# A batched matrix product: stores in 6 KB pieces, matmuls half by half in every group, and five stores queued behind the last load

## The chip, the cores and the metric

The kernel runs on one core of a Trainium2 chip. The metric is device time in microseconds (us) of one execution, the median of several runs. A profile of one execution shows what each engine did: TensorE (PE) multiplies, VectorE (DVE) and ScalarE (ACT) work on elements, and SyncE (SP) issues the transfers (DMAs) between HBM and the on-chip memory SBUF, which 16 DMA engines carry out.

## The reference

```python
dim: batch 32, i 256, j 512, k 384, all float32
def reference(x, y):        # x [32, 256, 512], y [32, 512, 384]
    return np.einsum('bij,bjk->bik', x, y).astype(np.float32)
```

So 32 independent products of a 256 x 512 matrix by a 512 x 384 matrix. Read are 16.8 MB of x and 25.2 MB of y, written are 12.6 MB.

## The kernel before

The 32 batches go in N = 8 groups of Q = 4. In SBUF each batch of a group has 32 of the 128 partitions. x arrives with 8 rows of a batch in each partition (16 KB in one piece), y with 16 rows (24 KB in one piece); only the y of the last group is loaded in four parts, with pieces of 6 KB.

A group goes through these steps. `transpose_x` casts x to float16 on VectorE (L83) and transposes it in 32 x 32 blocks of 4-byte words, two float16 values each (L90, L96). `round_y` casts y to float16 on VectorE in four parts of four rows (L102). `multiply` runs 128 matmuls (L113): the four batches lie on four row strips of TensorE, each sums over 16 steps t, and a group has two halves e (128 of the 256 output rows). Each half of a batch has a PSUM bank of its own, so a group uses all eight. `collect` copies a bank to the output tile (L128), and `store` writes that tile to HBM (L137).

The width decides the layout of the output. With WIDE, in groups 0 to 5, a batch has 32 output partitions with 8 output rows each: one store of 1.5 MiB a group, in pieces of 12 KB, and four copies of 32 partitions for each bank. With NARROW, in groups 6 and 7, a batch has 64 partitions with 4 rows: two stores of 0.75 MiB a group, in pieces of 6 KB, and two copies of 64 partitions for each bank.

In the wide groups the first half is multiplied in full, then the second, and ScalarE copies behind each half, except the last bank, whose copies VectorE makes in the next group. In groups 6 and 7 the halves alternate by quarters of t, and the copies follow at the end, on ScalarE; half of those of group 7 are on VectorE.

All loads and stores are issued from SP, in the order in which the program writes them. There are two buffers each for x, for the transposed x, for y and for the rounded y, and five for the output (DEFER + 2). A load waits until the buffer that it overwrites has been read: x(n+3) for the cast of x(n+1), y(n+2) for the rounding of y(n). The order of each engine is the program's order (`keep`). Around the end SP issues: x6, y5 and S2 (the store of group 2), x7, y6 and S3, y7 and S4, then S5, S6, S7.

Of the kernel before, what the change touches and what calls it, by code (L numbers as in the profile page):

```python
# [1 line left out]

# [4 lines left out]


MM_DT = mybir.dt.float16
F32 = mybir.dt.float32  # L10
P = 128


Q = 4
WIDE = 32
NARROW = 64

DEFER = 3

STEP = 4  # L20


@with_exitstack
def kernel(
    ctx: ExitStack,
    tc: tile.TileContext,
    x: bass.AP,
    y: bass.AP,
    out: bass.AP,
):  # L30
    nc = tc.nc

    B, I, J = x.shape
    _, _, K = y.shape

    PQ = P // Q
    R = I // PQ
    T = J // PQ
    TW = T // 2
    NE = I // P  # L40
    N = B // Q

    x_pool = ctx.enter_context(tc.tile_pool(name="x_pool", bufs=2))
    y_pool = ctx.enter_context(tc.tile_pool(name="y_pool", bufs=2))
    xr_pool = ctx.enter_context(tc.tile_pool(name="xr_pool", bufs=1))
    xt_pool = ctx.enter_context(tc.tile_pool(name="xt_pool", bufs=2))
    yr_pool = ctx.enter_context(tc.tile_pool(name="yr_pool", bufs=2))
    o_pool = ctx.enter_context(tc.tile_pool(name="o_pool", bufs=DEFER + 2))
    psum_pool = ctx.enter_context(
        tc.tile_pool(name="psum", bufs=2 * Q, space=bass.MemoryType.PSUM)  # L50
    )

    keep = tc.keep_in_program_order

    x_of, y_of, xt_of, yr_of, ps_of, o_of = {}, {}, {}, {}, {}, {}

    def width(n):
        return WIDE if n < N - 2 else NARROW  # L60

    def load_x(n):
        x_of[n] = x_pool.tile([P, R, J], F32, name="x_sb")
        keep(
            nc.sync.dma_start(
                out=x_of[n],
                in_=x[n * Q : (n + 1) * Q].rearrange("g (p r) j -> (g p) r j", r=R),
            )
        )

    def load_y(n):
        y_of[n] = y_pool.tile([P, T, K], F32, name="y_sb")
        src = y[n * Q : (n + 1) * Q].rearrange("g (q t) k -> (g q) t k", t=T)
        parts = 4 if n == N - 1 else 1
        for a in range(parts):
            s = slice(a * T // parts, (a + 1) * T // parts)
            keep(nc.sync.dma_start(out=y_of[n][:, s], in_=src[:, s]))

    def transpose_x(n):


        x_r = xr_pool.tile([P, R, J], MM_DT, name="x_r")
        keep(nc.vector.tensor_copy(x_r, x_of.pop(n)))  # L83
        xt_of[n] = xt_pool.tile([P, NE, TW, P], F32, name="xt_sb")
        words = x_r.bitcast(F32)
        if width(n) == WIDE:
            src = words.rearrange("p (h e) (q t) -> p e t h q", e=NE, t=TW)
            dst = xt_of[n].rearrange("p e t (h s) -> p e t h s", s=PQ)
            for e in range(NE):
                keep(nc.vector.transpose(dst[:, e], src[:, e]))  # L90
        else:
            src = words.rearrange("p (b h e) (q t) -> p b e t h q", b=2, e=NE, t=TW)
            dst = xt_of[n].rearrange("p e t (h s b) -> p b e t h s", s=PQ, b=2)
            for e in range(NE):
                for b in range(2):
                    keep(nc.vector.transpose(dst[:, b, e], src[:, b, e]))  # L96

    def round_y(n):
        y_sb = y_of.pop(n)
        yr_of[n] = yr_pool.tile([P, T, K], MM_DT, name="y_r")  # L100
        for a in range(0, T, STEP):
            keep(nc.vector.tensor_copy(yr_of[n][:, a : a + STEP], y_sb[:, a : a + STEP]))  # L102

    def multiply(n, e, first, last):
        xt = xt_of[n].bitcast(MM_DT).rearrange("p e t (m c) -> p e t m c", c=2)
        if first == 0:
            for g in range(Q):
                ps_of[n, e, g] = psum_pool.tile([P, K], F32, name="o_ps")
        for t in range(first, last):
            for g in range(Q):  # L110
                s = slice(g * PQ, (g + 1) * PQ)
                keep(
                    nc.tensor.matmul(  # L113
                        ps_of[n, e, g],
                        xt[s, e, t // 2, :, t % 2],
                        yr_of[n][s, t],
                        start=(t == 0),
                        stop=(t == T - 1),
                    )
                )  # L120

    def collect(copy, n, e, g):
        w = width(n)
        per = P // w
        ps = ps_of.pop((n, e, g))
        o = o_of[n].rearrange("p (u f) k -> p u f k", u=Q // per)
        for h in range(per):
            keep(copy(o[g % per * w : (g % per + 1) * w, g // per, h * NE + e], ps[h * w : (h + 1) * w]))  # L128

    def store(n):  # L130
        w = width(n)
        per = P // w
        o = o_of.pop(n).rearrange("p (u f) k -> p u f k", u=Q // per)
        for u in range(Q // per):
            b = n * Q + u * per
            keep(
                nc.sync.dma_start(  # L137
                    out=out[b : b + per].rearrange("g (s f) k -> (g s) f k", s=w),
                    in_=o[:, u],
                )  # L140
            )

    load_x(0)
    load_x(1)
    load_y(0)
    transpose_x(0)
    load_x(2)
    load_y(1)
    for n in range(N):
        if n + 1 < N:  # L150
            transpose_x(n + 1)
        if n > 0 and width(n - 1) == WIDE:
            collect(nc.vector.tensor_copy, n - 1, NE - 1, Q - 1)
        o_of[n] = o_pool.tile([P, R, K], F32, name="o_sb")
        round_y(n)
        if width(n) == WIDE:
            for e in range(NE):
                multiply(n, e, 0, T)
                for g in range(Q):
                    if (e, g) != (NE - 1, Q - 1):  # L160
                        collect(nc.scalar.copy, n, e, g)
        else:
            for a in range(0, T, STEP):
                for e in range(NE):
                    multiply(n, e, a, a + STEP)
            for u in range(2):
                for e in range(NE):
                    for v in range(2):
                        on_vector = n == N - 1 and v == 1
                        collect(nc.vector.tensor_copy if on_vector else nc.scalar.copy, n, e, 2 * u + v)  # L170
        if n + 3 < N:
            load_x(n + 3)
        if n + 2 < N:
            load_y(n + 2)
            if n + 2 - DEFER >= 0:
                store(n + 2 - DEFER)
    for n in range(N - DEFER, N):
        store(n)


# [1 line left out]
_INS = ['x', 'y']  # L182
_OUTS = [((32, 256, 384), 'float32')]


# [23 lines left out]
```

## Time and profile before

| | |
|---|---|
| time, median of 3 runs | 146.41 us (146.02 to 146.71) |
| the profiled execution: time, span of instructions | 145.94 us, 144.2 us |
| VectorE, ScalarE, matmuls busy | 95.7, 91.5, 63.7 us |
| moved by DMA | read 41.94 MB, written 12.58 MB |

The span runs from the first to the last instruction; the 1.7 us between it and the time lie around it. Times in the rows below are counted from the span's start. The granted clock of TensorE was 0.784 of full speed over the span.

### The profile page before, as it was taken

What the parts mean: (1) busy time and instruction counts of PE and PEld (TensorE: products, weight loads), DVE (VectorE), ACT (ScalarE), POOL (GpSimd) and SP (SyncE); (2) the same over time, 40 slices, a digit from 0 to 9 for tenths busy, and PEclk for the clock granted to TensorE, in tenths of its full rate; (3) what the DMA queues carried; (4) which work ended last, traced back from release to release, by engine and by line L of the source; (5) the groups of instructions that cost most, each with busy time, mean ns of one, the idle gap of its engine ahead of it and who ended that gap; (6) DMA issues with size and microseconds to landing.
All of it is one profiled execution on the core that took longest, in us unless ns stands there. A gap on an engine that the chain in (4) does not pass through costs nothing. (4 is left out here: it accounts for less than half of the span.)

```text
span 144.2 us, 2454 instructions
## 1 busy us (share of the span) xinstructions
PE 63.7 (44%) x1024; PEld 35.7 (25%) x1024; DVE 95.7 (66%) x92; ACT 91.5 (63%) x193; POOL 0.2 (0%) x4
## 2 busy tenths in 40 slices
PE   0000009930693059206960396029900499459700
PEld 0000005610361036103530153015600255115400
DVE  0069997669965997699639992998289980000470
ACT  3000000499969998999499969996799902980450
POOL 0000000000000000000000000000000000000000
PEclk9999999997589659955599569755796559955995
DMA  5999999999999999999999999999999999155055
GB/s 127 423 427 452 430 423 452 436 400 425 450 430 411 448 425 372 426 427 446 436 402 436 452 436 393 441 436 434 416 415 416 426 431 414 77 218 218 5 218 218
DMA packets 4187, 54.68 MB, mean 379 GB/s; under 512 B 464, under 2 KB 464, under 8 KB 1488
## 3 DMA queue, kind: packets, MB, share of 16 engines
q1 hardware_dynamic: 4176, 54.53, 89.7%
q8 instruction: 8, 0.13, 0.4%
q14 instruction: 3, 0.02, 0.0%
HBM read 41.94 MB, written 12.58 MB: 378 GB/s over the span
## 5 line engine op out<-in xcount | busy, mean ns | idle before, releaser
L128 ACT COPY o_sb<-o_ps 32x384 f32<-32x384 f32 (+1 forms) x192 | 90.2, 470 | 46.9 <-PE o_ps L113 30.2
L113 PE MATMUL o_ps<-y_r,xt_sb 32*128 32x384 f16 x1024 | 63.7, 410 | 72.2 <-DVE y_r L102 66.9
L113 PEld LDWEIGHTS <-xt_sb 32*128 32x128 f16 x1024 | 35.7, 116 | 99.8 <-issue 63.7
L90 DVE STREAM_TRANSPOSE xt_sb<-x_r 128x1024 f32<-128x1024 f32 x12 | 23.4, 1990 | 10.5 <-PE o_ps L113 10.4
L128 DVE COPY o_sb<-o_ps 32x384 f32<-32x384 f32 (+1 forms) x32 | 17.8, 556 | 17.0 <-PE o_ps L113 16.5
L102 DVE CAST y_r<-y_sb 128x1536 f16<-128x1536 f32 x32 | 28.5, 953 | 0.5 <-DMA y_sb<-in_y_dram 0.3
L83 DVE CAST x_r<-x_sb 128x4096 f16<-128x4096 f32 x8 | 18.3, 2289 | 10.3 <-DMA x_sb<-in_x_dram 10.2
L96 DVE STREAM_TRANSPOSE xt_sb<-x_r 128x512 f32<-128x512 f32 x8 | 8.1, 1070 | 5.8 <-PE o_ps L113 5.8
L128 ACT ACT_TABLE_LOAD x1 | 1.3, 1283 | 0.7 <-PEq L193 0.7
L193 POOL MEMSET const-bfloat16-1.0<- 128x1 bf16 x1 | 0.1, 101 | 0.0
L193 POOL MEMSET const-uint8-127<- 128x1 uint8 x1 | 0.1, 101 | 0.0
L193 POOL MEMSET const-float32-0.0<- 128x1 f32 x1 | 0.1, 98 | 0.2 <-issue 0.2
L193 POOL MEMSET const-float32-1.0<- 128x1 f32 x1 | 0.1, 98 | 0.0
## 6 DMA issues: line engine op xcount, KB each, us to landing
y_sb<-in_y_dram SPq DMA_DIRECT2D x7, 3072.0 KB, 21.8
x_sb<-in_x_dram SPq DMA_DIRECT2D x8, 2048.0 KB, 22.5
out_dram<-o_sb SPq DMA_DIRECT2D x6, 1536.0 KB, 22.6
y_sb<-in_y_dram SPq DMA_DIRECT2D x4, 768.0 KB, 15.4
out_dram<-o_sb SPq DMA_DIRECT2D x4, 768.0 KB, 3.2
```

The costliest lines, as they stand in the source:

```text
L83: keep(nc.vector.tensor_copy(x_r, x_of.pop(n)))
L90: keep(nc.vector.transpose(dst[:, e], src[:, e]))
L96: keep(nc.vector.transpose(dst[:, b, e], src[:, b, e]))
L102: keep(nc.vector.tensor_copy(yr_of[n][:, a : a + STEP], y_sb[:, a : a + STEP]))
L113: nc.tensor.matmul(ps_of[n, e, g], xt[s, e, t // 2, :, t % 2], yr_of[n][s, t], start=(t == 0), stop=(t == T - 1),)
L128: keep(copy(o[g % per * w : (g % per + 1) * w, g // per, h * NE + e], ps[h * w : (h + 1) * w]))
L193: nc = _bacc.Bacc("TRN2", target_bir_lowering=False, num_devices=1)
```

## The change

A list of steps, PLAN, now gives the order of the whole program: x and y are the loads of a group, T the transposes, R the rounding, M the matmuls, C the copies on ScalarE, D those on VectorE, S the stores.

All groups use the layout with 64 partitions to a batch, so all stores go in two halves of 0.75 MiB with pieces of 6 KB, and each bank has two copies of 64 partitions. All copies are on ScalarE, except half of those of group 7. Every group, the last two as well, multiplies its first half in full (four banks), then its second (the other four), and copies in the same order.

S0 and S1 keep their places among the loads, S2 moves from ahead of x7 to behind y6, S3 from ahead of y7 to behind it. S3 to S7 follow y7 on SP's queue. The output has six buffers instead of five.

```diff
--- before.py
+++ after.py
 Q = 4
-WIDE = 32
-NARROW = 64
-
-DEFER = 3
-
 STEP = 4
+O_BUFS = 6
+WIDE_GROUPS = 0
+PLAN = """
+x0 x1 y0
+T0 x2 y1
+T1 R0 M0 C0 x3 y2
+T2 R1 M1 C1 x4 y3 S0
+T3 R2 M2 C2 x5 y4 S1
+T4 R3 M3 C3 x6 y5
+T5 R4 M4 C4 x7 y6 S2
+T6 R5 M5 C5 y7
+T7 R6 M6 C6 R7 M7 C7 D7 S3 S4 S5 S6 S7
+"""
...
-    o_pool = ctx.enter_context(tc.tile_pool(name="o_pool", bufs=DEFER + 2))
+    o_pool = ctx.enter_context(tc.tile_pool(name="o_pool", bufs=O_BUFS))
...
     def width(n):
-        return WIDE if n < N - 2 else NARROW
+        return PQ if n < WIDE_GROUPS else 2 * PQ
+
+    def on_vector(n, e, g):
+        if n < WIDE_GROUPS:
+            return (e, g) == (NE - 1, Q - 1)
+        return n == N - 1 and g % 2 == 1
...
-    def multiply(n, e, first, last):
-        xt = xt_of[n].bitcast(MM_DT).rearrange("p e t (m c) -> p e t m c", c=2)
-        if first == 0:
+    def multiply(n):
+        xt = xt_of.pop(n).bitcast(MM_DT).rearrange("p e t (m c) -> p e t m c", c=2)
+        y_r = yr_of.pop(n)
+        o_of[n] = o_pool.tile([P, R, K], F32, name="o_sb")
+        for e in range(NE):
             for g in range(Q):
                 ps_of[n, e, g] = psum_pool.tile([P, K], F32, name="o_ps")
-        for t in range(first, last):
-            for g in range(Q):
...
+            for t in range(T):
+                for g in range(Q):
...
-    def collect(copy, n, e, g):
+    def collect(n, vector):
         w = width(n)
         per = P // w
-        ps = ps_of.pop((n, e, g))
+        copy = nc.vector.tensor_copy if vector else nc.scalar.copy
         o = o_of[n].rearrange("p (u f) k -> p u f k", u=Q // per)
-        for h in range(per):
-            keep(copy(o[g % per * w : (g % per + 1) * w, g // per, h * NE + e], ps[h * w : (h + 1) * w]))
+        for e in range(NE):
+            for g in range(Q):
+                if on_vector(n, e, g) != vector:
+                    continue
+                ps = ps_of.pop((n, e, g))
+                a = g % per * w
+                for h in range(per):
+                    keep(copy(o[a : a + w, g // per, h * NE + e], ps[h * w : (h + 1) * w]))
...
-    for n in range(N):
...
-            for a in range(0, T, STEP):
-                for e in range(NE):
-                    multiply(n, e, a, a + STEP)
...
-        if n + 3 < N:
-            load_x(n + 3)
-        if n + 2 < N:
-            load_y(n + 2)
-            if n + 2 - DEFER >= 0:
-                store(n + 2 - DEFER)
-    for n in range(N - DEFER, N):
-        store(n)
+    parts = {
+        "x": load_x,
+        "y": load_y,
+        "T": transpose_x,
+        "R": round_y,
+        "M": multiply,
+        "C": lambda n: collect(n, False),
+        "D": lambda n: collect(n, True),
+        "S": store,
+    }
+    for step in PLAN.split():
+        parts[step[0]](int(step[1:]))
```

## Rows read from the trace of the kernel before

**Rows 1.** Page: engines' busy time, DMA share by slice, the queue's traffic.
```profile
PE 63.7 (44%) x1024; PEld 35.7 (25%) x1024; DVE 95.7 (66%) x92; ACT 91.5 (63%) x193; POOL 0.2 (0%) x4
...
DMA  5999999999999999999999999999999999155055
...
q1 hardware_dynamic: 4176, 54.53, 89.7%
```
**Rows 2.** Chain of waits that ended last: start us, us, what.
```profile
129.33 5.85 PE o_ps L113 x91
...
139.26 0.56 DVE o_sb L128
```
**Rows 3.** Windows: stretch, us, busy by engine (instructions), PEclk, DMA share, GB/s.
```profile
6.00:120.00 114.00, 51.77 (x850) 29.81 (x854) 91.21 (x84) 78.87 (x168) 0.00 (x0) 0.78 1.01 427
118.00:122.00 4.00, 4.00 (x82) 2.37 (x75) 0.76 (x1) 0.54 (x2) 0.00 (x0) 0.80 1.02 433
122.00:126.00 4.00, 1.73 (x22) 0.62 (x16) 0.00 (x0) 3.86 (x9) 0.00 (x0) 1.00 0.26 108
...
132.00:138.00 6.00, 3.93 (x81) 2.27 (x72) 2.67 (x5) 2.72 (x6) 0.00 (x0) 0.90 0.01 3
```
**Rows 4.** Timeline of one cycle: start us, us, instruction [idle before].
```profile
65.06 3.57 DVE L102 CAST y_r<-y_sb 128x1536 f16<-128x1536 f32 x4
...
66.17 8.12 PE L113 MATMUL o_ps<-y_r,xt_sb 32*128 32x384 f16 x128 [7.46 <-DVE y_r L102]
...
68.66 0.33 SPq L77 DMA_DIRECT2D y_sb<-in_y_dram  x1
...
71.48 9.66 ACT L128 COPY o_sb<-o_ps 32x384 f32<-32x384 f32 x20 [1.81 <-PE o_ps L113]
...
78.35 2.27 DVE L128 COPY o_sb<-o_ps 32x384 f32<-32x384 f32 x4
```
**Rows 5.** Timeline of SP: three issues of DMAs.
```profile
84.24 0.33 SPq L77 DMA_DIRECT2D y_sb<-in_y_dram  x1
...
115.42 0.34 SPq L137 DMA_DIRECT2D out_dram<-o_sb  x1
...
139.89 0.33 SPq L137 DMA_DIRECT2D out_dram<-o_sb  x1
```
**Rows 6.** DMAs issued at 68.66, 84.24, 115.42, 139.89: KB, us to landing.
```profile
y_sb<-in_y_dram SPq DMA_DIRECT2D x1, 3072.0 KB, 22.2
...
y_sb<-in_y_dram SPq DMA_DIRECT2D x1, 3072.0 KB, 22.4
...
out_dram<-o_sb SPq DMA_DIRECT2D x1, 1536.0 KB, 9.7
...
out_dram<-o_sb SPq DMA_DIRECT2D x1, 768.0 KB, 3.3
```
**Rows 7.** Timeline of the last two groups.
```profile
117.80 0.96 DVE L102 CAST y_r<-y_sb 128x1536 f16<-128x1536 f32 x1 [0.35 <-DMA y_sb<-in_y_dram]
121.45 7.82 ACT L128 COPY o_sb<-o_ps 64x384 f32<-64x384 f32 x16 [6.06 <-issue]
```
**Rows 8.** Windows while a half store of group 6 moves alone.
```profile
126.50:127.00 0.50, 0.36 (x1) 0.00 (x0) 0.00 (x0) 0.49 (x2) 0.00 (x0) 0.50 1.06 442
127.00:127.50 0.50, 0.13 (x1) 0.10 (x1) 0.00 (x0) 0.47 (x2) 0.00 (x0) 0.50 1.05 430
```
**Rows 9.** By line and shape: busy us, mean ns, idle before.
```profile
L128 ACT COPY o_sb<-o_ps 32x384 f32<-32x384 f32 x168 | 78.9, 469 | 34.5 <-PE o_ps L113 30.2 <-issue 2.0
...
L90 DVE STREAM_TRANSPOSE xt_sb<-x_r 128x1024 f32<-128x1024 f32 x12 | 23.4, 1990 | 10.5 <-PE o_ps L113 10.4
...
L128 ACT COPY o_sb<-o_ps 64x384 f32<-64x384 f32 x24 | 11.3, 473 | 12.3 <-issue 12.0
L96 DVE STREAM_TRANSPOSE xt_sb<-x_r 128x512 f32<-128x512 f32 x8 | 8.1, 1070 | 5.8 <-PE o_ps L113 5.8
L128 DVE COPY o_sb<-o_ps 64x384 f32<-64x384 f32 x8 | 4.5, 556 | 16.6 <-PE o_ps L113 16.5
```

More of the change, by code (lines that the diff above doesn't have):

```diff
@@ L73, in load_y @@
         src = y[n * Q : (n + 1) * Q].rearrange("g (q t) k -> (g q) t k", t=T)
[L74 to L77, printed above, removed]
+        step = STEP if n == N - 1 else T
+        for a in range(0, T, step):
+            keep(nc.sync.dma_start(out=y_of[n][:, a : a + step], in_=src[:, a : a + step]))
     def transpose_x(n):
@@ L102, in round_y @@
             keep(nc.vector.tensor_copy(yr_of[n][:, a : a + STEP], y_sb[:, a : a + STEP]))
-    def multiply(n, e, first, last):
-        xt = xt_of[n].bitcast(MM_DT).rearrange("p e t (m c) -> p e t m c", c=2)
-        if first == 0:
+    def multiply(n):
[3 more added lines that the diff above has]
+        for e in range(NE):
             for g in range(Q):
                 ps_of[n, e, g] = psum_pool.tile([P, K], F32, name="o_ps")
-        for t in range(first, last):
-            for g in range(Q):
[L111 to L118, printed above, removed]
-                    )
-                )
-    def collect(copy, n, e, g):
+            for t in range(T):
+                for g in range(Q):
+                    s = slice(g * PQ, (g + 1) * PQ)
+                    keep(
+                        nc.tensor.matmul(
+                            ps_of[n, e, g],
+                            xt[s, e, t // 2, :, t % 2],
+                            y_r[s, t],
+                            start=(t == 0),
+                            stop=(t == T - 1),
+                        )
+                    )
+    def collect(n, vector):
         w = width(n)
         per = P // w
-        ps = ps_of.pop((n, e, g))
+        copy = nc.vector.tensor_copy if vector else nc.scalar.copy
         o = o_of[n].rearrange("p (u f) k -> p u f k", u=Q // per)
-        for h in range(per):
-            keep(copy(o[g % per * w : (g % per + 1) * w, g // per, h * NE + e], ps[h * w : (h + 1) * w]))
+        for e in range(NE):
+            for g in range(Q):
[5 more added lines that the diff above has]
+                    keep(copy(o[a : a + w, g // per, h * NE + e], ps[h * w : (h + 1) * w]))
     def store(n):
@@ L141, in store @@
             )
[L143 to L148, printed above, removed]
-    for n in range(N):
[L150 to L162, printed above, removed]
-            for a in range(0, T, STEP):
-                for e in range(NE):
-                    multiply(n, e, a, a + STEP)
[L166 to L170, printed above, removed]
-        if n + 3 < N:
-            load_x(n + 3)
-        if n + 2 < N:
-            load_y(n + 2)
-            if n + 2 - DEFER >= 0:
-                store(n + 2 - DEFER)
-    for n in range(N - DEFER, N):
-        store(n)
+    parts = {
[10 more added lines that the diff above has]
+        parts[step[0]](int(step[1:]))
 _INS = ['x', 'y']
```

16 lines of the change are left out of this document (5 added, 11 removed).

## The prediction

> **What bounds the kernel now.** I read the page's engine shares and slices first, then the chain of waits, then windows of the DMA share, then one cycle of the timeline. The page shows no engine above 66% of the span, while the row of DMA slices stands at 9 from the second slice to the 34th and at 1, 5, 5, 0, 5, 5 in the last six; the one queue in use moves 54.53 MB [rows 1]. So for 34 slices the transfers are the limit, and in the last six something else is. The chain of waits names it: the last 91 matmuls (129.33 to 135.18), then the copies of the last outputs, up to 139.26 + 0.56 = 139.8 [rows 2].
>
> The windows put numbers to it: from 6 to 120 the 16 DMA engines are busy for the whole time at 427 GB/s; from 122 on they move 0.26 of the time, and from 132 to 138 nothing [rows 3]. The transfers have run out of work there, because the stores of groups 6 and 7 wait for the copies of the last two groups. In these two windows alone 0.74 x 4 + 0.99 x 6 = 8.9 us of DMA time lie idle, all of it behind the end of the loads. In the middle of the run the engines keep pace: in the cycle shown VectorE goes from one rounding of y (65.06) to the next after the spare copy (78.35 + 2.27) in 15.6 us [rows 4], and group n loads and stores 2.10 + 3.15 + 1.57 = 6.82 MB, which at 427 GB/s take 16.0 us. (KB of the views are 1024 bytes: x is 2.10 MB a group, y 3.15, a store 1.57, half a store 0.786.)
>
> **The queue as a timetable.** Issue plus time to landing gives the landings [rows 5, 6]: y5 68.66 + 22.2 = 90.9; y6 84.24 + 22.4 = 106.6; the store of group 5 115.42 + 9.7 = 125.1; the last half of group 7 139.89 + 3.3 = 143.2. The last quarter of y7 lands just before 117.8, where VectorE's last rounding starts after a wait of 0.35 us for it [rows 7]. Bytes in issue order at 427 GB/s explain the distances: y5 to y6 has S2, x7, y6, 6.82 MB, 16.0 us (15.7 read); y6 to y7 has S3 and y7, 4.72 MB, 11.1 us (11.2 read); y7 to S5 has S4 and S5, 3.15 MB, 7.4 us (7.3 read). The queue works in the order of issue, each piece at its bytes. I use this for the new order.
>
> **The change part by part.**
> *Stores of groups 3 to 7 behind y7, S2 behind y6.* No byte is added. Ahead of y6 stands one store less: 106.6 - 3.7 = 102.9. Between y6 and the end of y7 stand S2 and y7 as S3 and y7 did: 102.9 + 11.1 = 114.0. Then follow five stores, and the queue has work up to the last of them if each is issued in time. SP issues in order, so behind y7 (which waits for the end of R5, about 95) stand S3 and S4, whose copies are long done, and S5, S6, S7, which wait for their copies. No load is left behind these waits. Earlier loads are issued no later than before: y(n+2) still waits for the rounding of group n, which comes earlier, and has some 22 us of queue ahead of it [rows 6]. Six more store issues on SP (16 for 10) at 0.33 us each [rows 5] hide behind that queue. The sixth output buffer means that group 6 waits for S0 and group 7 for S1, both landed long before: nothing.
>
> *6 KB stores for all groups.* The bytes stay, the pieces halve. The nearest rows are the half stores of group 6, alone in the queue: 442 and 430 GB/s at a share of 1.06 and 1.05 [rows 8], that is 417 and 410 at full share, mean 414; the 12 KB stores of groups 4 and 5 ran at 433 with a share of 1.02 [rows 3], 425 at full share. A store then takes 1.573/0.414 = 3.8 us for 3.7. Bounds: no dearer than 12 KB (3.7), or, at the lower of those half-microseconds and some dilution, 3.9. I take 3.8, the same operation.
>
> A rule of the Trainium skill speaks against this part: DMA: Bandwidth & Descriptors, section Rules for kernel authors, asks for at least 1 MiB per DMA for maximum bandwidth, and the halves here are 0.75 MiB; its section Measured gives 341 GB/s at 1 MB, by which ten halves would take, as an estimate, 23 us for the 19 below. The 433 GB/s [rows 3] are of whole stores, and no row has half stores queued behind each other, so the rule is kept as the second rival.
>
> *Copies and transposes.* Six groups change from 32 copies of 32 partitions (28 on ScalarE at 469 ns, 4 on VectorE) to 16 copies of 64 at 473 ns, all on ScalarE [rows 9]: ScalarE 13.5 to 7.6 us a group, VectorE loses 2.27 [rows 4]. Transposes go from 2 x 1.99 to at most 4 x 1.07 = 4.3 us [rows 9], 0.3 more. All this lies beside the queue and is worth nothing while the transfers are the limit. It matters only through the question whether the copies come in time.
>
> *Is the last group in time?* VectorE's cycle in the rows of the slowest matmuls: matmuls start 1.1 after the rounding, last 8.1, then the transposes of the group after next, 4.3 [rows 4, 9]: 13.6 us where now it is 15.6. R5 starts with y5's landing, 90.9; R6 at the later of 102.9 and 90.9 + 13.6 = 104.5. M6 runs from 105.6 to 113.7. Its first copy comes 5.3 us after its start as in rows 4 (66.17, 71.48), 110.9, and 16 copies at 0.473 end at 118.5. The first half of M7 uses banks that the first half of C6 has freed, and waits for y7: last rounding 114.0 + 1.0 = 115.0. The second half needs the last bank of C6, 118.5, takes half of 8.1, 122.6, and its copies, the slower ones 4 x 0.556 on VectorE, end at 124.8. The last half of S7 has its turn when all before it has landed, 114.0 + 4 x 3.8 + 1.9 = 131.1; it lands at 133.0, and with 3.3 from issue to landing it must be issued by 129.7. It has 4.9 us to spare. So the whole of the last group's matmuls and copies is hidden; if it came later than 129.7, each us would cost one.
>
> **The sum.** Last landing after: 114.0 + 5 x 3.8 = 133.0, and S0 to S2 at 0.08 more each, 0.2: 133.2. Before: 143.2. Gain 10.0 us. The profiled execution took 145.94 (a span of 144.2 and 1.7 around it), so 135.9; it lay 0.47 under the median of 146.41, so on that scale 136.4. What remains behind the landing (143.2 to 144.2) is unchanged. With 12 KB prices the last landing is 114.0 + 18.4 = 132.4, time 135.6. One more gain is open: the engines' work on the long queue is spent at about 123.0 (0.26 of the 4 us from 122 on [rows 3]), yet S5 lands at 125.1, so some engines end late; were they evened out in the store-only stretch, up to 1.2 us more: 134.4. With 3.9 a store and 0.2 x 3 more ahead, 134.1 and 137.3. The likeliest case's own range is 134.4 to 137.4.
>
> **Rivals.**
> *1. The last group comes late (smaller gain).* Now the last copy ends 139.8 - (117.8 + 0.96) = 21.1 us after the last rounding [rows 2, 7]. If the banks gate group 7 as they do now, the last copy comes at 115.0 + 21.1 = 136.1 and the last half lands at 136.1 + 0.1 + 3.3 = 139.5: 142.2 by the profiled run, 142.7 as a median. For it: same engines, same two groups at the end. Against it: of the 21.1 us, 7.8 are the copies of group 6, which start at 121.45 only after the whole of its matmuls [rows 7], and the last 91 matmuls wait for them to 129.33 [rows 2]; in cycles that go half by half, copies start 5.3 us into the matmuls [rows 4]. Chance 0.09, counting partial delays.
>
> *2. Half stores don't overlap (slower).* Each half store from issue to landing takes 3.3 us alone [rows 6]. If the store-only end pays that for every half in series, ten take 33 us: 114.0 + 33 = 147.0 for 143.2, 149.7 by the profiled run, 150.2 as a median. It decides from (143.2 - 114.0)/10 = 2.9 us a half, where 1.9 is forecast. For it: the lone halves are the only 6 KB stores in the trace. Against it: S4 and S5 ran back to back at 433 GB/s [rows 3], and y7, four DMAs of this same size and 6 KB pieces, passed the queue at the common rate (11.2 us read, 11.1 by bytes). Chance 0.04.
>
> **Chances and range.** Forecast 0.87, rival 1 0.09, rival 2 0.04. A difference under 0.5% is about what can't be told from none here; it takes a delay of nearly the whole gain, 0.02 out of rival 1. Faster 0.94, same 0.02, slower 0.04. The range starts at 134.4 and reaches into rival 1, to 138.6.
>
> **What the new profile would show.** Right: DMA slices at 9 to the last one or two; y7's last landing near 114; the last copy before 129; the chain that ends last made of store transfers, not of matmuls or copies; about 1.9 us between landings of half stores. Wrong: idle DMA between 114 and the end with SP waiting for copies (rival 1), a rate well under 400 GB/s in the store-only stretch (rival 2), or y7 landing later than 114 because a load was issued late in the middle of the run.

## The result and the profile after

The changed kernel takes 136.02 us (median of 5 runs, 136.0 to 136.76); the kernel before 146.41 (145.23 to 146.71). The ratio is 0.932, 95% interval 0.928 to 0.937. The forecast was 136.4, range 134.4 to 138.6. The profiled execution took 136.0, its span is 134.2. All ratios below are of runs in the faster of the two states that executions of one kernel fall into; medians and ranges are of all runs.

The page of the changed kernel, its engines' busy time, DMA slices and queue, against [rows 1]:

```profile
PE 59.7 (44%) x1024; PEld 34.8 (26%) x1024; DVE 83.5 (62%) x80; ACT 58.0 (43%) x121; POOL 0.2 (0%) x4
...
DMA  5999999999999999999999999999999999999991
...
q1 hardware_dynamic: 5040, 54.53, 96.8%
```

The 9s now reach the last slice but one, and the queue's share rises from 89.7% to 96.8% with the same 54.53 MB. No engine got busier; ScalarE fell from 91.5 to 58.0 us. The windows of the same kernel (stretch, us, busy by engine, granted clock, DMA share, GB/s), against [rows 3]:

```profile
6.00:120.00 114.00, 59.45 (x1024) 34.84 (x1024) 81.29 (x76) 54.84 (x116) 0.00 (x0) 0.82 1.01 424
118.00:122.00 4.00, 2.22 (x53) 1.35 (x45) 2.70 (x6) 3.18 (x7) 0.00 (x0) 1.00 1.03 427
122.00:126.00 4.00, 0.00 (x0) 0.00 (x0) 0.43 (x1) 0.05 (x1) 0.00 (x0) 0.57 0.99 413
126.00:130.00 4.00, 0.00 (x0) 0.00 (x0) 0.00 (x0) 0.00 (x0) 0.00 (x0) 0.50 1.01 422
130.00:131.00 1.00, 0.00 (x0) 0.00 (x0) 0.00 (x0) 0.00 (x0) 0.00 (x0) 0.50 0.80 332
131.00:131.50 0.50, 0.00 (x0) 0.00 (x0) 0.00 (x0) 0.00 (x0) 0.00 (x0) 0.50 0.47 197
...
132.00:132.50 0.50, 0.00 (x0) 0.00 (x0) 0.00 (x0) 0.00 (x0) 0.00 (x0) 0.50 0.21 86
```

In place of 0.26 from 122 to 126 there are 0.99 and 1.01 up to 130. Then the mean share of the 16 DMA engines falls in steps over some 2.5 us, as it does when they end one after another.

The timeline of group 6 before (rounding and matmuls), and then of the last two groups after, against [rows 4, 7]:

```profile
111.28 6.17 DVE L102 CAST y_r<-y_sb 128x1536 f16<-128x1536 f32 x7
...
112.39 1.78 PE L113 MATMUL o_ps<-y_r,xt_sb 32*128 32x384 f16 x18 [7.58 <-DVE y_r L102]
...
115.45 6.73 PE L113 MATMUL o_ps<-y_r,xt_sb 32*128 32x384 f16 x110 [1.28 <-ACT o_sb L128]
```

```profile
103.54 3.57 DVE L113 CAST y_r<-y_sb 128x1536 f16<-128x1536 f32 x4 [0.35 <-DMA y_sb<-in_y_dram]
...
104.65 7.62 PE L126 MATMUL o_ps<-y_r,xt_sb 32*128 32x384 f16 x130 [5.62 <-DVE y_r L113]
...
109.58 9.78 ACT L147 COPY o_sb<-o_ps 64x384 f32<-64x384 f32 x20 [5.29 <-issue]
...
114.69 0.96 DVE L113 CAST y_r<-y_sb 128x1536 f16<-128x1536 f32 x1 [0.90 <-DMA y_sb<-in_y_dram]
...
120.14 2.28 DVE L147 COPY o_sb<-o_ps 64x384 f32<-64x384 f32 x4 [1.23 <-PE o_ps L126]
```

Group 6 is rounded from 103.54 (111.28 in the profile before), its copies begin at 109.58, 4.9 us after its matmuls began (before, 9.1 us after: 112.39 to 121.45, when they were all but over); the last rounding of y7 starts at 114.69 (117.80), and the last copies end at 120.14 + 2.28 = 122.4 (139.8). SP's last issue, and then its DMA's size and time to landing:

```profile
122.49 0.43 SPq L156 DMA_DIRECT2D out_dram<-o_sb  x1
```

```profile
out_dram<-o_sb SPq DMA_DIRECT2D x1, 768.0 KB, 10.7
```

It lands at 122.49 + 10.7 = 133.2 where before the last half landed at 143.2 [rows 5, 6]. The last half store waits for its turn in the queue: it lands 10.7 us after its issue, where before it took 3.3.

One view misleads here. The chain that ended last stops at the last instruction with a busy time, which is now 11.8 us before the span's end:

```profile
95.94 18.73 DMA y_sb<-in_y_dram
...
117.46 2.69 PE o_ps L126 x60
...
121.87 0.56 DVE o_sb L147
```

Its last pieces are matmuls and copies that the last half store waits for, but that store then has 10.7 us of queue before it, so they do not set the end. The prediction said that this chain would end in store transfers; it can't, since it is followed back from the last copy. That the transfers set the end is read from the windows and the landing.

### The profile page after: what moved, and what is told of

It is laid out like the page before. It is cut to its first block, busy times and chain, and to the rows that moved or that the text cites. A ratio compares the mean times of both kernels' runs of the same rounds, so it can differ in the third digit from the quotient of the medians.

```text
span 134.2 us, 2377 instructions
## 1 busy us (share of the span) xinstructions
PE 59.7 (44%) x1024; PEld 34.8 (26%) x1024; DVE 83.5 (62%) x80; ACT 58.0 (43%) x121; POOL 0.2 (0%) x4
## 3 DMA queue, kind: packets, MB, share of 16 engines
q1 hardware_dynamic: 5040, 54.53, 96.8%
## 4 chain that ended last, share of the span: by engine, by line
DMA 57%; DVE 13%; PE 12%; ACT 7%; SPq 1%; issue 1%; DVEq 0%
DMA y_sb<-in_y_dram 51%; PE o_ps L126 12%; ACT o_sb L147 7%; DVE y_r L113 7%; DMA x_sb<-in_x_dram 6%; DVE xt_sb L107 3%; DVE x_r L100 2%; DVE o_sb L147 1%; SPq L94 1%; DVEq L199 0%; SPq L83 0%
## 5 line engine op out<-in xcount | busy, mean ns | idle before, releaser
L126 PE MATMUL o_ps<-y_r,xt_sb 32*128 32x384 f16 x1024 | 59.7, 398 | 60.6 <-DVE y_r L113 53.7
L147 ACT COPY o_sb<-o_ps 64x384 f32<-64x384 f32 x120 | 56.7, 473 | 63.3 <-PE o_ps L126 56.1
L126 PEld LDWEIGHTS <-xt_sb 32*128 32x128 f16 x1024 | 34.8, 113 | 85.0 <-issue 50.6
L107 DVE STREAM_TRANSPOSE xt_sb<-x_r 128x512 f32<-128x512 f32 x32 | 32.3, 1068 | 8.5 <-PE o_ps L126 8.2
L147 DVE COPY o_sb<-o_ps 64x384 f32<-64x384 f32 x8 | 4.5, 556 | 2.3 <-PE o_ps L126 2.2
```

Source lines behind the costliest of these rows:

```text
L107: keep(nc.vector.transpose(dst[:, c, e], src[:, c, e]))
L126: nc.tensor.matmul(ps_of[n, e, g], xt[s, e, t // 2, :, t % 2], y_r[s, t], start=(t == 0), stop=(t == T - 1),)
L147: keep(copy(o[a : a + w, g // per, h * NE + e], ps[h * w : (h + 1) * w]))
```

## The experiments

The change has three parts that can be made alone: the store places, the 6 KB layout of groups 0 to 5, and the half-by-half order of groups 6 and 7. The theory was that only the empty queue counts: the time is that of the transfers, plus what the last half store is issued later than 129.7 us. All edits are shown against the changed kernel. Each run is compared with the kernel before on the same chip (145.65, 145.88 or 146.08 there).

**Old store places, the rest as changed.**

```diff
-T4 R3 M3 C3 x6 y5
-T5 R4 M4 C4 x7 y6 S2
-T6 R5 M5 C5 y7
-T7 R6 M6 C6 R7 M7 C7 D7 S3 S4 S5 S6 S7
+T4 R3 M3 C3 x6 y5 S2
+T5 R4 M4 C4 x7 y6 S3
+T6 R5 M5 C5 y7 S4
+T7 R6 M6 C6 R7 M7 C7 D7 S5 S6 S7
```

> The changed kernel with S2 and S3 put back to their old places among the loads and S4 ahead of the rest, so that only S5 to S7 follow y7; 6 KB stores and half-by-half matmuls stay. Theory (the gain is only that the DMA queue no longer runs empty, whatever fills it): y7's last rounding moves back by one store, from 114.7 to about 118.5, the last copy from 122.4 to about 126.2; the last half store needs to be issued by 133 - 3.3 = 129.7, so the queue still has no gap and the time stays 136.0 (135.5 to 136.8). Rival (the stores deferred behind the last load carry the gain): most of the 10 us is lost, 142 or more.

Measured 136.69 us (136.57 to 137.15), ratio 0.940 (0.935 to 0.944). The last copy ends at 126.5, still in time. The rival, that the deferral carries the gain, falls: with the other two parts there, the store places are worth 0.7 us by the medians and 1.1 by the ratios (on different chips; the intervals overlap).

**12 KB stores in groups 0 to 5, the rest as changed.**

```diff
-WIDE_GROUPS = 0
+WIDE_GROUPS = 6
...
-T2 R1 M1 C1 x4 y3 S0
...
+T2 D0 R1 M1 C1 x4 y3 S0
...
```

The lines after it get their D step in the same way: the spare copies, those of each wide group's last bank, which VectorE makes in the next group.

> The changed kernel with 12 KB stores, 32-partition copies and the spare copy on VectorE in groups 0 to 5 as before; the new order and half-by-half matmuls of the last groups stay. Theory: VectorE's cycle is some 2 us longer but hidden; the six stores come back to 12 KB, 0 to 0.5 us less: 135.4 to 136.2. Rival (the cheaper copies of the 6 KB layout carry a part): the last group comes late and the time is above 138.

Measured 136.32 us (135.19 to 136.66), ratio 0.935 (0.929 to 0.941): no difference from the changed kernel, and no sign of the gain from larger stores. Its timeline, the rounding of group 6 and the last copies, and a window near the end:

```profile
110.87 7.04 DVE L113 CAST y_r<-y_sb 128x1536 f16<-128x1536 f32 x8
...
127.11 2.28 DVE L147 COPY o_sb<-o_ps 64x384 f32<-64x384 f32 x4 [1.60 <-PE o_ps L126]
```

```profile
126.00:130.00 4.00, 1.18 (x29) 0.57 (x19) 2.22 (x4) 2.23 (x5) 0.00 (x0) 0.89 0.65 262
```

VectorE starts group 6 at 110.87, not 103.54, without a wait before it: its cycle has the spare copies again. The last copy ends at 129.4, just at the bound of 129.7. But the queue is not full up to there: from 126 to 130 the DMA engines are busy for 0.65 of the time, 1.4 us lost, where the changed kernel has 1.01. The larger stores and the late copies about cancel; no full kernel here has 12 KB stores with early copies.

**Only the last two groups half by half.** This is the 12 KB edit above with the stores in their old places, so it does what the kernel before does but for the order of groups 6 and 7 (and a sixth output buffer):

```diff
-WIDE_GROUPS = 0
+WIDE_GROUPS = 6
...
+T4 D2 R3 M3 C3 x6 y5 S2
+T5 D3 R4 M4 C4 x7 y6 S3
+T6 D4 R5 M5 C5 y7 S4
+T7 D5 R6 M6 C6 R7 M7 C7 D7 S5 S6 S7
...
```

> The kernel before, with nothing changed but that groups 6 and 7 are multiplied and copied half by half (and a sixth output buffer): 12 KB stores in groups 0 to 5 and old places of all stores. Theory: group 6 is rounded at 111.3 as before, its last copies end near 126, the second half of group 7 ends near 128.5 and its copies near 130.7, so the last half store is issued about 1 us after the 129.7 that it would need: 136 to 138. Rival (deferral carries the gain): 144 to 146.

Measured 136.06 us (135.57 to 137.28), ratio 0.937 (0.931 to 0.942). This part alone brings a gain that can't be told from the whole (0.932, intervals overlapping). The timeline, rounding and matmuls of group 6, the copies behind them, the last copies, and the same window as above:

```profile
110.20 5.30 DVE L113 CAST y_r<-y_sb 128x1536 f16<-128x1536 f32 x6
...
111.30 7.25 PE L126 MATMUL o_ps<-y_r,xt_sb 32*128 32x384 f16 x130 [7.58 <-DVE y_r L113]
115.86 9.80 ACT L147 COPY o_sb<-o_ps 64x384 f32<-64x384 f32 x20 [1.33 <-issue]
...
126.43 2.28 DVE L147 COPY o_sb<-o_ps 64x384 f32<-64x384 f32 x4 [1.60 <-PE o_ps L126]
```

```profile
126.00:130.00 4.00, 0.50 (x13) 0.09 (x1) 2.22 (x4) 1.90 (x4) 0.00 (x0) 0.81 0.71 290
```

Group 6 starts hardly earlier than before (110.20 for 111.28), but its copies begin 4.6 us into its matmuls, where before they began 9.1 us into them, at 121.45 [rows 7]. The last copy ends at 128.7, 11.1 us earlier than before and inside the bound; I had reckoned 130.7. Here too the queue runs partly dry, 0.71 from 126 to 130: this kernel reaches the same time with larger stores and some idle DMA time, not with a queue that is full to the end.

**Quarters back in the last two groups, the rest as changed.**

```diff
-        for e in range(NE):
-            for g in range(Q):
+        step = STEP if n >= N - 2 else T
+        for a, e in [(a, e) for a in range(0, T, step) for e in range(NE)]:
+            for g in range(Q if a == 0 else 0):
...
-            for t in range(T):
+            for t in range(a, a + step):
...
+        if n >= N - 2:
+            order = [(e, 2 * u + v) for u in range(2) for e in range(NE) for v in range(2)]
...
```

> The changed kernel with the last two groups multiplied by quarters of t with both halves alternating, and copied afterwards in the old order, as before; new store places and 6 KB stores stay. Theory: the copies of group 6 start only after all its matmuls, 112.3, and end at 120.2; group 7's matmuls wait for them bank by bank, end near 126.5, its copies near 131.2; the last half is issued some 1.5 us late: 137 to 139.5. Rival (deferral alone carries the gain): 136.0. Rival (the half-by-half order carries it): 143 or more.

Measured 136.45 us (135.95 to 137.76), ratio 0.938 (0.933 to 0.944); the profiled execution is the slowest of them, 137.76.

```profile
104.25 3.53 DVE L113 CAST y_r<-y_sb 128x1536 f16<-128x1536 f32 x4
...
113.05 7.84 ACT L150 COPY o_sb<-o_ps 64x384 f32<-64x384 f32 x16 [7.87 <-issue]
...
126.96 4.56 DVE L150 COPY o_sb<-o_ps 64x384 f32<-64x384 f32 x8 [10.98 <-PE o_ps L127]
```

The copies of group 6 begin at 113.05, 7.7 us after its matmuls (105.32), and the last copies end at 131.5, 1.8 us past the bound; that execution is 1.8 us above the changed kernel's. In the median, deferral with the 6 KB layout comes to within 0.4 us of it without the half-by-half order (ratios 0.938 and 0.932, intervals overlapping). So two ways lead to nearly the same time, and either suffices.

**Only the 6 KB layout, and only the store places.**

Both have the edit that brings the quarters back, shown just above. The layout alone has with it the old store places (the edit of the first run), the store places alone the 12 KB layout with the spare copies (the edit of the second run).

> Of the change only the 6 KB layout (stores, copies of 64 partitions, no spare copy on VectorE) in all groups; old store places, and the last two groups by quarters as before. Theory (what counts is when the last copy comes, against about 130, and that is the start of group 6 plus the tail of the last two groups): VectorE starts group 6 at 107.7 instead of 111.3, its matmuls end near 117, the copies behind them near 125, group 7's matmuls near 131, the last copy near 135.4, landing 3.4 later: 141 to 141.7, about half of the gain. Rival (any one part fills the queue, as each run so far did): 136 to 136.7. Rival (the layout is worth nothing by itself): 145 or more.

Measured 139.86 us (138.85 to 141.12), ratio 0.961 (0.955 to 0.967): six tenths of the gain, and 1.1 us below the lower end of the 141 to 141.7 expected. The timeline of group 6's rounding, its copies, and the last copies:

```profile
108.00 3.57 DVE L113 CAST y_r<-y_sb 128x1536 f16<-128x1536 f32 x4 [1.26 <-DMA y_sb<-in_y_dram]
...
115.99 7.83 ACT L150 COPY o_sb<-o_ps 64x384 f32<-64x384 f32 x16 [10.88 <-issue]
...
129.46 4.56 DVE L150 COPY o_sb<-o_ps 64x384 f32<-64x384 f32 x8 [8.78 <-PE o_ps L127]
```

VectorE without the spare copies is ready for group 6 before y6 has landed (it waits 1.26 us for it) and starts it at 108.00 (111.28 before). The old tail, from there to the last copy, follows to 134.0; it takes 26.0 us, where before it took 28.5 and the expectation counted 27.7.

> Of the change only the store places (S2 behind y6, S3 to S7 behind y7); 12 KB layout in groups 0 to 5 and the last two groups by quarters as before. Theory: VectorE starts group 6 at 110.9, as with the 12 KB layout in the run before, so the earlier landing of y6 and y7 is not used, and the same tail of 28.5 us follows (111.3 to 139.8 before): last copy near 139.4, 145 to 146.4, no gain. Rival (deferral alone carries the gain): 136 to 137.

Measured 145.91 us (144.34 to 146.87, 12 runs), ratio 0.998 (0.993 to 1.003): no gain, as expected. Moving stores behind the last load lets y6 land earlier, but with the 12 KB layout VectorE is not there to use it: it reaches group 6 at 110.40 with no wait for y6, and in the 12 KB run above, with the same loads, at 110.87.

**Transfers alone.** Is anything but the transfers left in 136 us? (For the 12 KB run, WIDE_GROUPS = 8.)

```diff
-    parts = {
...
+    def fill(n):
+        o_of[n] = o_pool.tile([P, R, K], F32, name="o_sb")
+        keep(nc.vector.memset(o_of[n], 1.0))
+
+    skip = lambda n: None
+    parts = {"x": load_x, "y": load_y, "T": skip, "R": skip, "M": fill, "C": skip, "D": skip, "S": store}
```

> Only the transfers of the changed kernel in their order, stores of 6 KB; the casts, transposes, matmuls and copies are left out, and each output tile is filled with ones once. Theory: the changed kernel has nothing left but its transfers, so 135.3 to 136.2. Rival (the computation still costs something, by waits of loads for VectorE or by engines that end late): 134.5 or less.

> The same transfers alone with 12 KB stores in all groups (8 stores of 1.5 MiB); all computation left out as in the run before. The price of the smaller pieces by itself: the prediction took 0.08 us a store, 0.6 us over eight stores; bounds 0 to 1.0. So 0 to 1.0 us below the 6 KB run, 0.6 expected.

Measured 135.89 us (135.44 to 136.14) for 6 KB in 16 DMAs, ratio 0.936 (0.932 to 0.941), and 134.49 (134.31 to 135.03) for 12 KB in 8 DMAs, ratio 0.927 (0.923 to 0.932). The first agrees with the changed kernel (0.932, intervals overlapping): its computation is hidden as far as these runs can tell. The second shows what the smaller pieces in more DMAs cost: 1.4 us, above the bound of 1.0. Windows of the 6 KB run, then of the 12 KB run:

```profile
6.00:120.00 114.00, 16.97 (x7) 0.00 (x0) 1.00 1.01 423
128.00:130.00 2.00, 0.00 (x0) 0.00 (x0) 1.00 1.00 418
130.00:131.00 1.00, 0.00 (x0) 0.00 (x0) 1.00 0.74 307
131.00:132.00 1.00, 0.00 (x0) 0.00 (x0) 1.00 0.44 184
```

```profile
6.00:120.00 114.00, 16.97 (x7) 0.00 (x0) 1.00 1.00 428
128.00:130.00 2.00, 0.00 (x0) 0.00 (x0) 1.00 0.88 375
130.00:131.00 1.00, 0.00 (x0) 0.00 (x0) 1.00 0.12 49
131.00:132.00 1.00, 0.00 (x0) 0.00 (x0) 1.00 0.00 0
```

With the smaller pieces the rate from 6 to 120 falls from 428 to 423 GB/s, and the end is ragged: from 130 to 131 and from 131 to 132 the engines of the 6 KB run still move 0.74 and 0.44 of the time, those of the 12 KB run 0.12 and nothing. Two runs were to tell the size of the pieces from the number of DMAs:

6 KB pieces in one DMA a group, and 12 KB pieces (WIDE_GROUPS = 8) in two DMAs of 64 partitions, both with the computation left out as above:

```diff
+        if True:
+            dst = out[n * Q : (n + 1) * Q].rearrange("(u g) (s f) k -> (g s) u (f k)", u=Q // per, s=w)
+            keep(nc.sync.dma_start(out=dst, in_=o.rearrange("p u f k -> p u (f k)")))
+            return
```

```diff
-            keep(
...
+            dst = out[b : b + per].rearrange("g (s f) k -> (g s) f k", s=w)
+            for p in range(0, P, P // 2):
+                keep(nc.sync.dma_start(out=dst[p : p + P // 2], in_=o[p : p + P // 2, u]))
```

> Transfers alone again, 6 KB pieces, but one DMA of 1.5 MiB a group instead of two of 0.75 MiB; all computation left out. 12 KB in 8 DMAs took 134.49, 6 KB in 16 took 135.89. If the piece size has the price: 135.9. If the number of DMAs has it: 134.5.

> Transfers alone, 12 KB pieces, but each store in two DMAs of 64 partitions (0.75 MiB); all computation left out. If the piece size has the price: 134.5. If the number of DMAs has it: 135.9.

Measured 135.03 us (134.64 to 135.16), ratio 0.928 (0.923 to 0.934), and 138.23 (137.57 to 138.8), ratio 0.951 (0.945 to 0.956). Windows of the first, then of the second:

```profile
6.00:120.00 114.00, 16.97 (x7) 0.00 (x0) 1.00 1.01 427
...
130.00:131.00 1.00, 0.00 (x0) 0.00 (x0) 1.00 0.30 123
131.00:132.00 1.00, 0.00 (x0) 0.00 (x0) 1.00 0.06 25
```

```profile
60.00:112.00 52.00, 5.24 (x2) 0.00 (x0) 1.00 1.00 408
...
132.00:134.00 2.00, 0.00 (x0) 0.00 (x0) 1.00 0.51 215
```

6 KB pieces in 8 DMAs come near the 12 KB run, at 427 GB/s with a short end. This speaks for the number of DMAs as most of the price, and so does the stretch from 60 to 112 us of the four traces: 429 and 428 GB/s with 8 DMAs (12 KB, 6 KB), 420 and 408 with 16 (6 KB, 12 KB). But the two pairs ran on different chips, the intervals of the ratios for 16 and 8 DMAs still touch (0.932 to 0.934), and the second run neither agrees with one price nor the other: stores of 64 partitions are dearer than both, with some engines still at work from 132 to 134. It was a bad control, since it also halves the partitions. How the 1.4 us divides stays open.

**12 KB in groups 0 to 5 without the spare copies on VectorE.** An attempt at a better version.

```diff
-WIDE_GROUPS = 0
+WIDE_GROUPS = 6
...
-        if n < WIDE_GROUPS:
-            return (e, g) == (NE - 1, Q - 1)
         return n == N - 1 and g % 2 == 1
```

> The changed kernel with the 12 KB layout in groups 0 to 5, all of their 32 copies on ScalarE (15 us a group), so that VectorE has no spare copies. Theory: the transfers are the limit, 12 KB in six groups takes three quarters of the 1.4 us off, and VectorE starts group 6 near 104 as in the changed kernel, so the last copy stays before 126: 134.7 to 135.3. Rival (ScalarE with 15 us a group becomes late): 136 or more.

Measured 139.88 us (139.27 to 141.07), ratio 0.963 (0.957 to 0.969). The theory's number fell, the rival's came. The timeline: ScalarE's copies from group 0 on in one piece, then the matmuls of the second half of group 5 with their wait, the transposes behind them, the rounding of group 6:

```profile
26.98 102.74 ACT L145 COPY o_sb<-o_ps 32x384 f32<-32x384 f32 x212 [24.97 <-PE o_ps L124]
...
104.48 4.43 PE L124 MATMUL o_ps<-y_r,xt_sb 32*128 32x384 f16 x61 [1.62 <-ACT o_sb L145]
...
108.95 4.04 DVE L105 STREAM_TRANSPOSE xt_sb<-x_r 128x512 f32<-128x512 f32 x4 [7.49 <-PE o_ps L124]
112.90 7.01 DVE L111 CAST y_r<-y_sb 128x1536 f16<-128x1536 f32 x8
```

ScalarE copies without a pause from 26.98 to 129.7. The matmuls wait for their banks (1.62 us in this line), the transposes for the matmuls (7.49 us), and group 6 starts at 112.90; the last copy ends at 132.8. I had counted 15 us a group against the transfers' 16 and so took ScalarE for the quicker; read are 102.74/212 = 0.485 us a copy, 15.5 us a group. And between y5 and y6 there is no store, the loads need only 12.3 us, and an engine with no pause can't make up what it is behind. That last step is argued from these numbers, not tested.

**One DMA a group in the changed kernel** (the edit of the 6 KB, 8 DMA run, for groups 0 to 6).

> The changed kernel with 6 KB pieces as they are, but the stores of groups 0 to 6 in one DMA of 1.5 MiB each; group 7 keeps two halves. If the piece size has the price of 1.4 us: 136.0, no change. If the number of DMAs has it: 134.7 to 135.0.

Measured 135.62 us (135.33 to 135.96), ratio 0.933 (0.928 to 0.938). It lies 0.4 us under the changed kernel's median, but the ratios are the same within their intervals and the two were not run side by side: not shown to be better.

## Why the prediction was right

*The queue as a timetable* held to 0.7 us. y6 was to land at 102.9; it was issued at 78.70 and landed 24.8 us later, at 103.5. y7 was to land at 114.0; its last rounding starts at 114.69 after 0.90 us of waiting for it. The last landing was to be at 133.2 and is at 133.2. That this agrees to 0.1 us is luck, since two errors met. The loads came 0.6 us late: the timetable took a whole store, 3.7, off the 15.7 us read between y5 and y6 and so left 12.0, where x7 and y6 need 12.3 by their bytes and took 103.5 - 91.0 = 12.5. And the five stores behind y7 took 133.2 - 114.6 = 18.6 us, 3.7 each and not 3.8. The profiled execution was to take 135.9 and took 136.0; the 0.47 us added for the median did not come again.

*The last group in time.* Group 6 was reckoned to start at 104.5 and the last copy to end at 124.8; read are 103.54 and 122.4. The 104.5 was VectorE's cycle (its terms add up to 13.5, not 13.6); in the run VectorE was ready first and waited 0.35 us for y6. The bound of 129.7 us for the last half store, and one us lost for each beyond, can be checked on the profiled executions, all of which have 6 KB stores in groups 6 and 7:

| | last copy ends | past 129.7 | time | above 136.0 |
|---|---|---|---|---|
| changed kernel | 122.4 | - | 136.0 | - |
| one DMA a group | 122.6 | - | 136.0 | 0.0 |
| old store places | 126.5 | - | 136.6 | 0.6 |
| only halves | 128.7 | - | 135.6 | -0.4 |
| 12 KB in 0 to 5 | 129.4 | - | 136.3 | 0.3 |
| quarters back | 131.5 | 1.8 | 137.8 | 1.8 |
| 12 KB, all on ScalarE | 132.8 | 3.1 | 140.0 | 4.0 |
| only the layout | 134.0 | 4.3 | 140.2 | 4.2 |
| before | 139.8 | 10.1 | 145.9 | 9.9 |
| only the store places | 140.7 | 11.0 | 146.9 | 10.9 |

Nine of the 10 executions fall on that line within 0.6 us, and the transfers alone (135.8) lie at its foot; the run with all copies on ScalarE, where the stores before the last came late as well (the DMA share is 0.70 from 118 to 122 and 0.62 from 122 to 126), lies 0.9 above it. This is the mechanism, and it is shown. What each part does to it can be read from one distance, from group 6's rounding to the last copy: 18.5 to 19.9 us in the six kernels with the half-by-half order, 26.0 to 30.3 in the four with quarters.

*Copies and transposes* were called worth nothing while the transfers are the limit. In the changed kernel that is so only in the sum (12 KB back: no difference in time, but the last copy came at 129.4 instead of 122.4 and the queue ran partly dry). Taken alone the layout is worth 0.039 of the time, because before, the end was not set by the transfers: it hung on the start of group 6, which VectorE's cycle sets. Of the 5.8 us that the last copy gained, 3.3 are that start and 2.5 the shorter tail.

*Half stores.* Rival 2 is out: from 122 to 130 they ran back to back at 413 and 422 GB/s, and the ten behind y7 took 18.6/10 = 1.86 us each, where 1.9 was forecast and the rival needed 2.9. The rule of the Trainium skill (DMA: Bandwidth & Descriptors, section Rules for kernel authors: at least 1 MiB per DMA) has the right sign here, if the number of DMAs is what costs the 1.4 us, which stays open. The 341 GB/s behind the prediction's 23 us stand in the Trainium skill (DMA: Bandwidth & Descriptors, section Measured) for loads issued from GpSimd; the ten half stores here, issued from SP, took 18.6 us. The prediction's term for the price was mis-sized: 0.08 us a store was taken, 1.4/8 = 0.18 measured. The stretch with stores alone does not show it; in the transfers alone it lies in the mixed stretch from 60 to 112 us (420 for 429 GB/s) and in the ragged end. The gain of up to 1.2 us that the lower end of the range took for engines that end evenly has no working beside it, and it did not come: their mean share fell over 2.5 us.

*Rival 1* was priced too high. It carried the 21.1 us from the last rounding of y to the last copy over to the new order; that distance was not a property of the tail. The tail hangs on group 6: from its rounding to the last copy it took 28.5 us before, 27.3 with quarters back and 26.0 with the layout only. With group 6 at 104.25 the quarters cost 1.8 us in one execution and 0.4 in the median, not the 6.3 us (142.2 for 135.9) of the rival.

*What the prediction did not see* is that the parts overlap. It priced the change as a whole; the runs show that the half-by-half order alone gives a ratio of 0.937, deferral with the layout 0.938, the layout alone 0.961, deferral alone 0.998. The part that the sum was written around, the stores behind the last load, brings nothing by itself.

## What to carry to other kernels

Where the transfers fill the run but not its end, reckon two times: when the queue would have moved its bytes, and when the last store can be issued; here the time followed the later one, and each edit that brought the second near the first was worth about the same, so one of them was enough. The queue here worked in order of issue and could be forecast as a list of bytes over one rate, to 0.7 us. Before a step is moved earlier, look at which engine will not be there to use it.

## What the runs showed of the hardware that was not expected

SP's waits before the stores in the changed kernel (us in total, times, longest):

```profile
SPq L156 <- DMA y_sb<-in_y_dram: 11.1, 4, 6.7
...
SPq L156 <- DVE o_sb L147: 4.3, 2, 3.5
SPq L156 <- ACT o_sb L147: 4.2, 2, 2.6
SPq L156 <- DMA out_dram<-o_sb: 2.9, 2, 1.5
```

Of the waits of these store issues 14.0 us are for the landing of earlier DMAs and 8.5 for copies. The longest, 6.7 us, is for y6: the second half of S3 is issued at 103.58, just after y6 lands at 103.5, and y6 is the eighth DMA before it. The next five stores wait in the same way for the two halves of S2 and the first three parts of y7, each the eighth before. The trace records the landings of all 35 DMAs on eight semaphores, and all six waits end with the landing of the eighth DMA before. So at most eight are under way at once in this program. Here the eight under way, half stores of 6.3 MB in all or 15 us, were enough of a queue. Eight stores of half the size would be half of that, as an estimate by the same count; no run here shows it.

Stores of 64 partitions took 2.3 us more over the run than as many DMAs of the same bytes with 128 partitions and half the piece (138.23 for 135.89, on different chips; ratios 0.951 and 0.936, intervals apart). It is not their own rate: while they moved alone, from 120 to 128 us, they ran at 429 GB/s, and the 6 KB stores at 427. The rate was lower from 60 to 112 (408 for 420) and the end longer. And after a long queue the 16 engines do not end together: the mean share of the changed kernel's fell over some 2.5 us, that of the 12 KB transfers alone over about 1.5 (from 129.5 to 131).
